# Gate columns moved behind the first two chunk batches, chunk preparation opened on other memory, in a hybrid GDN/retention block on one core

## The chip, the cores and the metric

One core of one Trainium2 chip. The metric is the time of one execution on the device, in microseconds. The engines are TensorE (PE in the profile; PEld are its weight loads), VectorE (DVE), ScalarE (ACT), GpSimd (POOL) and SyncE (SP, which here only issues transfers). Each engine runs its own instructions in order; a scheduler that works at build time has put them in that order, from a model of the engines.

## The reference

One layer, D_MODEL 1024, 1024 latent tokens behind 256 context tokens, all in float32. The modulated, normalized tokens h go through one input projection, whose columns are split; the first half of the heads is a bidirectional gated delta rule (GDN), the second half retention with rotary embedding:

```python
p = (h @ w_in).astype(f32)
qkv_a, z, ab, rq, rk, rv, rg = jnp.split(p, splits, axis=-1)
qkv_a = short_conv(qkv_a, cw)                  # 5 taps, then silu
q = l2_normalize(q) * (HEAD_DIM ** -0.5);  k = l2_normalize(k)
g_f = -A[0] * jax.nn.softplus(a_f + dtb[0])    # and g_b, backward
o_f = gated_delta_rule(q, k, v, g_f, jax.nn.sigmoid(b_f))
...
G = jnp.cumsum(gc, axis=-1)                    # in each chunk
A = jnp.where(strict, jnp.einsum('nbhid,nbhjd->nbhij', kb, kc) * decay, 0.0)
sol = lax.linalg.triangular_solve(A + I, rhs, lower=True, unit_diagonal=True)
...
o_gdn = rms_norm(o_f + o_b) * jax.nn.silu(z)
o_ret = head_group_norm(r_f + r_b) * jax.nn.silu(rg)
x = x + g1 * (y @ w_out);  x = x + g2 * swiglu(modulate(rms_norm(x), sh2, sc2))
```

The gates g1, g2 and the shifts and scales come from adaLN: silu(c) times a 1024 x 6144 matrix. After it a final RMSNorm.

## The kernel before, in words

**Tiles.** The 1280 tokens are ten tiles of 128, two of context and eight latent (LT = 8, TT = 10). h lies in SBUF transposed, as hhi and hlo, its fp32r parts; each product of the projection is three matmuls (hhi·whi, hhi·wlo, hlo·whi). *Token-major* columns (`token_major`, L371 to L373) come in ten groups of 256 columns, 24 matmuls per token tile; the result is emptied into a buffer res by `finish` and stored (L387). Groups 0, 1 are the retention values rv, 2 to 5 rk and rq (rope), 6, 7 the gate columns rg (emptied with a Silu, `fin_gate`, L532), 8, 9 the columns z. *Channel-major* columns (`conv_block`, L611 to L613) are twelve heads of 128 for GDN: 4 to 7 k, 0 to 3 q, 8 to 11 v. One head has chunks of 256, 512 and 512 tokens, each 24 matmuls into a bank of PSUM of the two that are called b (b2 in the program); ScalarE empties each twice, into u and, times the middle tap, into y (L614, L615); VectorE adds the other taps (L621); a Silu ends it (L624).

**The order of the program** around the change: rv; `ada_rest(2, half)` for both halves; the gates chain; four k heads, each with an `ada_rest` and `kstat`; four q heads, the first two with an `ada_rest`; gate columns; chunk batches 0 and 1 (`solve`); four v heads; batch 2; the merges; z. `ada_rest` makes 512 columns of adaLN: four loads of 512 KB (adaw2, two buffers, SP's queue, L495), eight products on VectorE into acc (L497, L499), then a matmul gr (L504 or L509). The gates chain is: av from xa (the 16 gate columns of rv's group 0), softplus, g, the prefix sums G by a matmul with the triangle tri (L582, L583), its transpose GT (L595), neG, gl and kds by three exponentials (L589 to L593), and the store of G to memory as grow_d.

`solve(b)` runs `pre(t)` for the tiles of a batch and then `invert(b)`. `pre` loads the head's keys kc and queries qc from memory (SP), makes kk (L705), the transposed query qt (L710) and kq (L715) on PE, loads G's rows (gw), masks them on GpSimd, puts them through Exp, multiplies (ut, sp on VectorE) and stores both. `invert` inverts the 32 x 32 triangular blocks of a batch row by row on VectorE (X, tmp; L765, L767) and stores the blocks (xd, L771). `merge` (L807, L814 and others; tile m) loads them into U and t (L787, L788) and puts the blocks together with small matmuls. The v heads are turned by PE (vT, L856), scaled on ScalarE into vt (L859, two buffers) and stored.

**Memory.** Pools are opened and closed on two stacks, so what opens later lies on what was closed. Pool W (two buffers) holds the weights of the convolutions and of groups 0, 8 and 9; pool W2 the weights of groups 1, 6 and 7, xa, and the four result buffers of rv; R2 holds the buffers of `ada_rest` and `kstat`; GU, GI and GP those of the chunk preparation and the inverses. Before, W2 and R2 both live from the value columns until the gate columns are done, and GU, GI and GP open behind them (L685 to L693).

Of the kernel before, what the change touches and what calls it, by code (L numbers as in the profile page):

```python
# [17 lines left out]
P = 128  # L18
# [5 lines left out]
TT = NTOK // P  # L24
# [14 lines left out]
def build(nc, tc, ap, dbg=None, stop=None, marks=None):  # L39
    root = ExitStack()  # L40
    V, S, G, T, SY = nc.vector, nc.scalar, nc.gpsimd, nc.tensor, nc.sync

    def pool(name, bufs=1, side=None, space=None):
        kw = {}
        if side is not None:
            kw["side"] = side
        if space is not None:
            kw["space"] = space
        if space is not DRAM:
            kw["reuse_waits"] = "tile"  # L50
# [8 lines left out]
    def close(p):  # L59
        p_close.pop(id(p)).close()  # L60
# [29 lines left out]
    def bank_a(name):  # L90
        return bank("pa", name)

    def bank_b(name):
        return bank("pb", name)
# [96 lines left out]
    try:  # L191
# [20 lines left out]
        W = pool("w", bufs=2)  # L212
# [14 lines left out]
        xts, raws, small = {}, {}, {}  # L227
# [4 lines left out]
        W2 = None  # L232
# [127 lines left out]
        def tm_weights(g, kh, pl, q=S):  # L360
            return weights(ap["wt"][g, :, 4 * kh:4 * kh + 4, :], [4, 256], V, pl, q, raws.get((g, kh)), g == 0)

        def tm_bank(g):
            return bank_a("tm")[:, 0:WIDE if g == 0 else 256]

        def tm_half(o, w, kh, t):

            tsl = slice(t * P, (t + 1) * P)
            whi, wlo = w
            for k in range(4 * kh, 4 * kh + 4):  # L370
                T.matmul(o, hhi[:, k, tsl], whi[:, k % 4, :], start=(k == 0), stop=False)  # L371
                T.matmul(o, hhi[:, k, tsl], wlo[:, k % 4, :], start=False, stop=False)  # L372
                T.matmul(o, hlo[:, k, tsl], whi[:, k % 4, :], start=False, stop=(k == KT - 1))  # L373
# [5 lines left out]
        def tm_store(g, t, o, finish, store, pl):  # L379
            early = g < 2  # L380
            res = (W2 if early else R1).tile([P, 256], F32, tag="res", name="res", bufs=4 if early else 2)
            finish(t, o[:, 0:256], res)
            if g == 0:
                S.activation(xa[:, t, :], o[:, 256:WIDE], AF.Copy)
            nm, c0 = GROUPS[g // 2], (g % 2) * 256
            dst = zd[t - 2, :, c0:c0 + 256] if nm == "z" else rd[t, :, RD[nm], c0:c0 + 256]
            store.dma_start(dst, res)  # L387

        def token_major(g, tiles, finish, store, pl, q=S):

            w = [tm_weights(g, kh, pl, q) for kh in range(2)]

            for p in range(0, len(tiles), 2):
                pair = [(t, tm_bank(g)) for t in tiles[p:p + 2]]
                for kh in range(2):
                    for t, o in pair:
                        tm_half(o, w[kh], kh, t)
                for t, o in pair:
                    tm_store(g, t, o, finish, store, pl)
# [48 lines left out]
        W2 = pool("w2", bufs=2)  # L448
        xa = W2.tile([P, TT, 16], F32, tag="xa", name="xa", bufs=1)
# [31 lines left out]
        checkpoint("h")  # L481


        R2 = pool("r2", bufs=2)
        ada2 = C.tile([P, 2, KT], F32, tag="ada2", name="ada2")
        grow = [dr.tile([1, D], F32, tag="grow%d" % i, name="grow%d" % i) for i in range(2)]

        def ada_rest(c, half):

            c0 = c * D + half * 512  # L490
            acc = R2.tile([P, 512], F32, tag="acc", name="acc", bufs=1)
            for k in range(KT):
                if k % 2 == 0:
                    w = R2.tile([P, 2, 512], F32, tag="adaw2", name="adaw2", bufs=2)
                    SY.dma_start(w, ap["ada_w"][k * P:(k + 2) * P, c0:c0 + 512].rearrange("(a p) n -> p a n", p=P))  # L495
# [5 lines left out]
            if c in (2, 5):  # L501
                row = R2.tile([1, 512], F32, tag="row", name="row", bufs=1)
                SY.dma_start(row, ap["adarow"][c0:c0 + 512].unsqueeze(0))
# [12 lines left out]

        nA = R2.tile([P, 8], F32, tag="nA", name="nA", bufs=1)

# [15 lines left out]
        LAT, ALL = list(range(2, TT)), list(range(2, TT)) + [0, 1]  # L534
        for g in range(2):
# [1 line left out]
        checkpoint("rv")  # L537


        GS = pool("gs", side="right")  # L540
        sm = {n: GS.tile([P, TT * 8], F32, tag=n, name=n)
              for n in ("g", "G", "nG", "Gt", "neG", "gl", "beta", "ab", "kds")}
        nk = GS.tile([P, TT, H], F32, tag="nk", name="nk")
        nq = GS.tile([P, LT, H], F32, tag="nq", name="nq")
        cw = GS.tile([P, 12, 5], F32, tag="cw", name="cw")
        SY.dma_start(cw, ap["cw"])
# [8 lines left out]
        def c8(t, d):  # L555
            return slice(t * 8 + d * 4, t * 8 + d * 4 + 4)

        AB = pool("ab", side="right")
        tri = AB.tile([P, 2, P], F32, tag="tri", name="tri")
        SY.dma_start(tri, ap["tri"])  # L560
        CHUNKS = [(0, 256), (256, 512), (768, 512)]
        av = AB.tile([P, 2, TT * 8], F32, tag="av", name="av")
        av3 = av.rearrange("p a (t c) -> p a t c", c=8)
        V.tensor_tensor(av3[:, 0], xa[:, :, 0:8], bc(small["dtb"], [P, TT, 8], 1), ALU.add)
        V.tensor_scalar(av3[:, 1], xa[:, :, 8:16], -1.0, None, ALU.mult)
        S.activation(nA, small["alog"], AF.Exp)
        V.tensor_scalar(nA, nA, -1.0, None, ALU.mult)
        sp = softplus(AB, av.rearrange("p a n -> p (a n)"), 2 * TT * 8, "sp")

        lnb = GS.tile([P, TT, 2, H], F32, tag="lnb", name="lnb")  # L570
        V.tensor_scalar(lnb.rearrange("p t d h -> p (t d h)"), sp[:, TT * 8:], -1.0, None, ALU.mult)
# [1 line left out]
        V.tensor_tensor(sm["g"].rearrange("p (t c) -> p t c", c=8), sp.rearrange("p (t c) -> p t c", c=8),  # L573
                        bc(nA, [P, TT, 8], 1), ALU.mult)
        be = sm["beta"].rearrange("p (t c) -> p t c", c=8)
        S.activation(be, xa[:, :, 8:16], AF.Exp, scale=-1.0)
        V.tensor_scalar(sm["beta"], sm["beta"], 1.0, None, ALU.add)
        V.reciprocal(sm["beta"], sm["beta"])
        ps = bank_b("G")
# [15 lines left out]
        T.transpose(ps[:80, :P], sm["G"], ident)  # L595
        gT = AB.tile([80, P], F32, tag="gT", name="gT")
        V.tensor_copy(gT, ps[:80, :P])
        SY.dma_start(grow_d, gT)
        close(AB)
        CV = pool("cv", side="right")  # L600
# [25 lines left out]
        def newy():  # L626
            return CV.tile([P, NTOK], F32, tag="y", name="y", bufs=3)
# [3 lines left out]
        def kstat(h, y):  # L631

            cut = ((0, 4), (4, 4), (8, 2))
            ps = [bank_b("kt") for _ in cut]
            kts = [R2.tile([P, 2, 4, P], F32, tag="kt", name="kt", bufs=3) for _ in cut]
            for (t0, n), pt, kt in zip(cut, ps, kts):
# [4 lines left out]
            V.tensor_scalar(nk[:, :, h], nk[:, :, h], EPS, None, ALU.add)  # L641
            rk2 = R2.tile([P, TT], F32, tag="rk2", name="rk2", bufs=2)
            V.reciprocal(rk2, nk[:, :, h])
# [25 lines left out]

        lnk = log(GS, nkf, TT * H, "ln").rearrange("p (t h) -> p t h", h=H)  # L670
        nG4 = sm["nG"].rearrange("p (t d h) -> p t d h", d=2, h=H)
# [11 lines left out]
                        y[:, NCTX:].rearrange("p (t j) -> p t j", j=P))  # L683

        checkpoint("q")  # L685
        for g in (6, 7):
            token_major(g, LAT, fin_gate, S, W2, SY)
        checkpoint("rg")
        close(R2)
        close(W2)  # L690
        GU = pool("gu")
        GI = pool("gi")
        GP = pool("gp")  # L693
# [147 lines left out]
        def solve(b):  # L841
            for t in BATCH[b]:
                pre(t)
            checkpoint("pre%d" % b)
            invert(b)
            checkpoint("inv%d" % b)

        solve(0)
        solve(1)
        for h in range(H):  # L850
            y = newy()
            conv_block(8 + h, y, False)
            for t0, n in ((0, 2), (2, 4), (6, 4)):
                ps = bank_a("vT")
                for t in range(t0, t0 + n):
                    T.transpose(ps[:, (t - t0) * P:(t - t0 + 1) * P], y[:, t * P:(t + 1) * P], ident)  # L856
                vt = CV.tile([P, 4, P], F32, tag="vt", name="vt", bufs=2)
                for t in range(n):
                    S.activation(vt[:, t], ps[:, t * P:(t + 1) * P], AF.Copy, scale=sv3[:, t0 + t, h:h + 1])  # L859
                S.dma_start(vd[t0:t0 + n, :, h, :].rearrange("t p j -> p t j"), vt[:, :n])  # L860
# [687 lines left out]
        for m in (1, 6, 2, 7, 5, 4, 3):  # L1548
            gs = [list(range(j, min(j + 2, FH))) for j in range(4 if m == 1 else 0, FH, 2)]
# [103 lines left out]
```

## Time and profile before

| | us |
|---|---|
| three timed runs, median (range) | 1481.48 (1479.01 to 1484.4) |
| profiled execution, span | 1479.4 |
| PE busy in the span | 1400.0 (95%) |
| VectorE busy | 969.2 (66%) |
| ScalarE busy | 613.4 (41%) |
| GpSimd busy | 590.5 (40%) |

The times are those of three runs; of the profiled execution itself the profile gives the span, from the first to the last instruction. In a timeline a row is start, duration, engine, line of the kernel, operation, result <- operands, shapes, count, and in brackets the idle time ahead of it with what ended it. In the view of waits a row is the engine and its instruction, what it waited for, and the total, the number and the longest of those waits. "issue" stands where the profile shows nothing that was waited for.

### The profile page before, as it was taken

To read this page: it belongs to the slowest core of one execution; us is meant where nothing else is said; L and a number is where in the kernel's file an instruction comes from. 1 tells how busy PE (TensorE), PEld (TensorE's weight loads), DVE (VectorE), ACT (ScalarE), POOL (GpSimd) and SP (SyncE) were. 2 spreads that over 40 slices of the span, in tenths; PEclk is the share of its full clock that TensorE was granted. 3 is DMA by queue.
4 is the path that set the end of the run, shared out by engine and by line. 5 is a ranking of instruction groups with operands and counts; after the bars stand their busy time and mean duration, and the time that the engine had idled before them with its cause. 6 is when DMAs were issued, how large, how long until landed. Compare 5 with 4: busy or idle time off the path is not lost.

```text
span 1479.4 us, 24109 instructions
## 1 busy us (share of the span) xinstructions
PE 1400.0 (95%) x8919; PEld 1203.0 (81%) x8919; DVE 969.2 (66%) x1856; ACT 613.4 (41%) x1326; POOL 590.5 (40%) x501
## 2 busy tenths in 40 slices
PE   7999999987789999899699899999999999999997
PEld 2898888976789999799588688877888888788886
DVE  6566789289782535579777877646555564657577
ACT  5643564687333111245534533223333332444444
POOL 0120010243201354244144688899555553325321
PEclk9999999999899999999899999999999999999999
DMA  8536686688878723996633265765222242785863
GB/s 323 210 106 203 189 250 199 223 263 279 269 196 271 272 72 118 416 372 204 215 114 115 86 226 208 260 238 178 107 108 107 107 150 76 234 280 193 305 206 114
DMA packets 176565, 298.14 MB, mean 202 GB/s; under 512 B 43496, under 2 KB 93880, under 8 KB 172096
## 3 DMA queue, kind: packets, MB, share of 16 engines
q1 hardware_dynamic: 124896, 253.17, 49.7%
q10 hardware_dynamic: 49072, 35.83, 7.8%
q0 software_dynamic: 2480, 7.60, 1.4%
q8 instruction: 70, 1.15, 0.3%
q14 instruction: 47, 0.39, 0.1%
HBM read 206.60 MB, written 89.96 MB: 200 GB/s over the span
## 4 chain that ended last, share of the span: by engine, by line
PE 55%; POOL 6%; DMA 6%; issue 3%; DVE 2%; ACT 2%; SPq 0%; ACTq 0%; POOLq 0%; DVEq 0%
PE ffn L1344 7%; PE ffn L1342 6%; PE ffn L1343 6%; PE fo L1470 5%; PE fo L1468 5%; PE fo L1469 5%; PE tm L371 3%; PE tm L372 3%; PE tm L373 3%; PE op L1201 2%; PE op L1203 2%; PE op L1202 2%; DMA wd<-tw 1%; POOL ws L1315 1%; PE up L929 1%
## 5 line engine op out<-in xcount | busy, mean ns | idle before, releaser
L371 PE MATMUL tm<-whi,hhi 128*128 128x256 f32 (+1 forms) x704 | 201.5, 290 | 6.1 <-ACT vt L859 2.9
L372 PE MATMUL tm<-wlo,hhi 128*128 128x256 f32 (+1 forms) x704 | 200.8, 287 | 0.3 <-DVE wlo L345 0.3
L373 PE MATMUL tm<-whi,hlo 128*128 128x256 f32 (+1 forms) x704 | 198.6, 286 | 0.0
L371 PEld LDWEIGHTS tm<-whi,hhi 128*128 128x128 f32 x704 | 134.2, 192 | 10.3 <-ACT vt L859 3.1
L344 ACT ACTIVATE whi<-wraw 128x512 fp32r<-128x512 f32 (+2 forms) x98 | 75.2, 771 | 159.7 <-PE ffn L1343 81.9
L1344 PE MATMUL ffn<-t,wlo 128*128 128x512 f32 x352 | 137.1, 390 | 1.4 <-DVE wlo L345 1.4
L1342 PE MATMUL ffn<-t,whi 128*128 128x512 f32 x352 | 137.0, 390 | 1.3 <-ACT whi L344 1.3
L1343 PE MATMUL ffn<-t,whi 128*128 128x512 f32 x352 | 137.0, 389 | 0.0
L372 PEld LDWEIGHTS tm<-wlo,hhi 128*128 128x128 f32 x704 | 135.2, 192 | 2.2 <-issue 0.9
L373 PEld LDWEIGHTS tm<-whi,hlo 128*128 128x128 f32 x704 | 134.3, 192 | 0.7 <-DVE hlo L314 0.2
L344 ACT ACTIVATE whi<-ws 128x512 fp32r<-128x512 f32 x88 | 55.6, 632 | 173.0 <-PE ffn L1343 123.7
L345 DVE TENSOR_TENSOR wlo<-ws,whi 128x512 fp32r<-128x512 f32 x88 | 95.1, 1081 | 45.7 <-ACT whi L344 45.3
L1468 PE MATMUL fo<-whi,ahi 128*128 128x512 f32 x308 | 119.3, 389 | 0.7 <-ACT ahi L344 0.7
L1469 PE MATMUL fo<-wlo,ahi 128*128 128x512 f32 x308 | 119.9, 389 | 0.0
L1470 PE MATMUL fo<-whi,alo 128*128 128x512 f32 x308 | 119.0, 390 | 0.0
L345 DVE TENSOR_TENSOR wlo<-wraw,whi 128x512 fp32r<-128x512 f32 (+2 forms) x92 | 103.4, 1125 | 23.4 <-ACT whi L344 23.2
L1342 PE MATMUL ffn<-b,whi 128*128 128x512 f32 x264 | 103.9, 394 | 4.3 <-ACT whi L344 4.3
L1344 PE MATMUL ffn<-b,wlo 128*128 128x512 f32 x264 | 103.7, 393 | 0.7 <-DVE wlo L345 0.7
L1343 PE MATMUL ffn<-b,whi 128*128 128x512 f32 x264 | 103.7, 393 | 0.0
L612 PE MATMUL b<-hlo,whi 128*128 128x512 f32 (+1 forms) x256 | 94.7, 370 | 0.0
L613 PE MATMUL b<-hhi,wlo 128*128 128x512 f32 (+1 forms) x256 | 94.5, 369 | 0.0
L611 PE MATMUL b<-hhi,whi 128*128 128x512 f32 (+1 forms) x256 | 94.2, 368 | 0.0
(446 smaller groups left out, 3443.7 us busy)
## 6 DMA issues: line engine op xcount, KB each, us to landing
adaw<-ada_w SPq DMA_DIRECT2D x48, 512.0 KB, 4.8
pk<-sd SPq DMA_DIRECT2D x16, 1536.0 KB, 11.6
wraw<-wfi SPq DMA_DIRECT2D x44, 512.0 KB, 3.9
ar<-ad SPq DMA_DIRECT2D x33, 512.0 KB, 4.8
w<-wfo SPq DMA_DIRECT2D x22, 512.0 KB, 5.7
wd<-tw SPq DMA_DIRECT2D x11, 1024.0 KB, 4.8
ad<-act SPq DMA_DIRECT2D x20, 512.0 KB, 3.1
raw<-wd SPq DMA_DIRECT2D x20, 512.0 KB, 4.9
```

What stands on the lines that cost most here:

```text
L344: S.activation(hi, raw, AF.Copy)
L345: e.tensor_tensor(lo, raw, hi.bitcast(F32), ALU.subtract)
L371: T.matmul(o, hhi[:, k, tsl], whi[:, k % 4, :], start=(k == 0), stop=False)
L372: T.matmul(o, hhi[:, k, tsl], wlo[:, k % 4, :], start=False, stop=False)
L373: T.matmul(o, hlo[:, k, tsl], whi[:, k % 4, :], start=False, stop=(k == KT - 1))
L612: T.matmul(o, whi[:, k, :], hl, start=False, stop=False)
L1342: T.matmul(o, whi[:, k, :], xhi(xn, slice(0, 4), k), start=(first and k == 0), stop=False, **kw)
L1343: T.matmul(o, whi[:, k, :], xlo(xn, slice(0, 4), k), start=False, stop=False, **kw)
L1344: T.matmul(o, wlo[:, k, :], xhi(xn, slice(0, 4), k), start=False, stop=(k == 3), **kw)
L1468: T.matmul(po[g][i], ahi[:, ts], whi, start=(j == 0 and not kw), stop=False, **kw)
L1469: T.matmul(po[g][i], ahi[:, ts], wlo, start=False, stop=False, **kw)
L1470: T.matmul(po[g][i], alo[:, ts], whi, start=False, stop=(j == FH - 1), **kw)
```

## The change

Three edits. First, the pools GS and AB open, and tri, av and its two operations stand, ahead of `ada_rest(2, ·)`; then W2 is closed, and R2 is opened behind that, so R2 lies where W2 was. The exponential for beta now reads av instead of xa, which is closed by then. Second, the two groups of gate columns go behind `solve(0)` and behind `solve(1)`, and take their weights from pool W instead of W2, still on SP's queue. Third, W2 is therefore not open when GU, GI and GP are opened; what these lie on has been free since the value columns, apart from what R2 covers.

```diff
+        GS = pool("gs", side="right")
+        AB = pool("ab", side="right")
+        tri = AB.tile([P, 2, P], F32, tag="tri", name="tri")
+        SY.dma_start(tri, ap["tri"])
+        av = AB.tile([P, 2, TT * 8], F32, tag="av", name="av")
...
+        V.tensor_tensor(av3[:, 0], xa[:, :, 0:8], bc(small["dtb"], [P, TT, 8], 1), ALU.add)
+        V.tensor_scalar(av3[:, 1], xa[:, :, 8:16], -1.0, None, ALU.mult)
+        close(W2)
         R2 = pool("r2", bufs=2)
...
-        S.activation(be, xa[:, :, 8:16], AF.Exp, scale=-1.0)
+        S.activation(be, av3[:, 1], AF.Exp)
...
         checkpoint("q")
-        for g in (6, 7):
-            token_major(g, LAT, fin_gate, S, W2, SY)
-        checkpoint("rg")
         close(R2)
-        close(W2)
         GU = pool("gu")
...
         solve(0)
+        token_major(6, LAT, fin_gate, S, W, SY)
         solve(1)
+        token_major(7, LAT, fin_gate, S, W, SY)
+        checkpoint("rg")
```

The scheduler orders all engines anew. Line numbers differ by a few: L611 to L613 of before are L612 to L614 after, L504 is L513, L582 is L583, L705 is L702, and so on.

The first place is PE in the first k head, behind its second chunk. The names are tm, a tile of gate columns; gr, the matmul that ends a half of `ada_rest(2, ·)`; G, the prefix sums; GT, G transposed; b2, a chunk of a convolution. Before, around the second gr:

```order
L371 MATMUL tm_2477<-whi_2409,hhi_86 128x256
L504 MATMUL gr_1273<-acc_1256,ones_81 1x512
L372 MATMUL tm_2477<-wlo_2410,hhi_86 128x256
L373 MATMUL tm_2477<-whi_2409,hlo_87 128x256
L371 MATMUL tm_2477<-whi_2409,hhi_86 128x256
L372 MATMUL tm_2477<-wlo_2410,hhi_86 128x256
L582 MATMUL G_1335<-g_1282,tri_1301 128x40 x2
L583 MATMUL G_1335<-g_1282,ones_81 128x80
```

After, from the end of the second chunk to the start of the third:

```order
L614 MATMUL b2_1393<-hhi_86,wlo_1360 128x512
L513 MATMUL gr_1262<-acc_1245,ones_81 1x512
L513 MATMUL gr_1285<-acc_1268,ones_81 1x512
L583 MATMUL G_1336<-g_1291,tri_1232 128x40 x2
L584 MATMUL G_1336<-g_1291,ones_81 128x80
L596 MATMUL GT_1349<-ident_65,G_1292 80x128
L612 MATMUL b2_1420<-hhi_86,whi_1359 128x512
```

Six tiles' worth of gate columns, 135 matmuls, stood between the second chunk and the third, and gr, G and GT were strewn among them; now both gr, G and GT follow one another, and no gate column is near.

The second place is SP's queue at the loads of adaLN columns for these two halves. adaw2 are the loads, row the adaLN bias and grow0 the finished half row. Before:

```order
L495 DMA adaw2_1234<-ada_w 128x2x512
L495 DMA adaw2_1238<-ada_w 128x2x512
L503 DMA row_1251<-adarow 1x512
L546 DMA cw_1293<-cw 128x60
L560 DMA tri_1301<-tri 128x256
L495 DMA adaw2_1242<-ada_w 128x2x512
L495 DMA adaw2_1246<-ada_w 128x2x512
L495 DMA adaw2_1257<-ada_w 128x2x512
L495 DMA adaw2_1261<-ada_w 128x2x512
L354 DMA wraw_2647<-wt 128x1024
```

After:

```order
L487 DMA tri_1232<-tri 128x256
L554 DMA cw_1302<-cw 128x60
L504 DMA adaw2_1246<-ada_w 128x2x512
L504 DMA adaw2_1250<-ada_w 128x2x512
L512 DMA row_1263<-adarow 1x512
L504 DMA adaw2_1254<-ada_w 128x2x512
L504 DMA adaw2_1258<-ada_w 128x2x512
L504 DMA adaw2_1269<-ada_w 128x2x512
L504 DMA adaw2_1273<-ada_w 128x2x512
```

The order of the loads is the same, and the loads of gate-column weights (wraw from wt) among them are gone; but the two buffers of adaw2 now lie where W2's weights and results were.

The third place is PE behind the last v head, where kk, qt and kq belong to the last two tiles of the third batch, vT to the last two v heads, and tm_4968 is the first tile of z. Before, from the last convolution matmul:

```order
L613 MATMUL b2_3980<-hhi_86,wlo_3920 128x512
L705 MATMUL kk_4055<-kc_4053 128x128 x3
L856 MATMUL vT_3889<-ident_65,y_3791 128x128 x2
L856 MATMUL vT_3896<-ident_65,y_3791 128x128 x4
L856 MATMUL vT_3907<-ident_65,y_3791 128x128 x4
L705 MATMUL kk_4055<-kc_4053 128x128
L710 MATMUL qt_4062<-ident_65,qc_4060 128x128 x4
L715 MATMUL kq_4071<-qc_4060,kc_4053 128x128 x4
L705 MATMUL kk_4114<-kc_4112 128x128 x4
L710 MATMUL qt_4121<-ident_65,qc_4119 128x128 x4
L715 MATMUL kq_4130<-qc_4119,kc_4112 128x128 x4
L856 MATMUL vT_4016<-ident_65,y_3918 128x128 x2
```

After:

```order
L614 MATMUL b2_3980<-hhi_86,wlo_3920 128x512
L707 MATMUL qt_4121<-ident_65,qc_4119 128x128 x4
L712 MATMUL kq_4130<-qc_4119,kc_4112 128x128
L856 MATMUL vT_3889<-ident_65,y_3791 128x128 x2
L856 MATMUL vT_3896<-ident_65,y_3791 128x128 x4
L856 MATMUL vT_3907<-ident_65,y_3791 128x128 x4
L712 MATMUL kq_4130<-qc_4119,kc_4112 128x128 x3
L856 MATMUL vT_4016<-ident_65,y_3918 128x128 x2
L856 MATMUL vT_4023<-ident_65,y_3918 128x128 x4
L856 MATMUL vT_4034<-ident_65,y_3918 128x128 x4
L371 MATMUL tm_4968<-whi_4956,hhi_86 128x256
```

Both kk, the first qt and the first kq have moved ahead into the convolutions; one qt, one kq and the vT of two heads are left behind the last convolution.

More of the change, by code (lines that the diff above doesn't have):

```diff
@@ L481, in build @@
         checkpoint("h")
+        GS = pool("gs", side="right")
[3 more added lines that the diff above has]
+        av = AB.tile([P, 2, TT * 8], F32, tag="av", name="av")
+        av3 = av.rearrange("p a (t c) -> p a t c", c=8)
+        V.tensor_tensor(av3[:, 0], xa[:, :, 0:8], bc(small["dtb"], [P, TT, 8], 1), ALU.add)
+        V.tensor_scalar(av3[:, 1], xa[:, :, 8:16], -1.0, None, ALU.mult)
+        close(W2)
         R2 = pool("r2", bufs=2)
@@ L537, in build @@
         checkpoint("rv")
-        GS = pool("gs", side="right")
         sm = {n: GS.tile([P, TT * 8], F32, tag=n, name=n)
@@ L556, in c8 @@
             return slice(t * 8 + d * 4, t * 8 + d * 4 + 4)
-        AB = pool("ab", side="right")
-        tri = AB.tile([P, 2, P], F32, tag="tri", name="tri")
-        SY.dma_start(tri, ap["tri"])
         CHUNKS = [(0, 256), (256, 512), (768, 512)]
[L562 to L565, printed above, removed]
         S.activation(nA, small["alog"], AF.Exp)
```

## Prediction

> **What bounds the kernel now.** I read the page first, then busy time by stage, then the waits of TensorE (PE), then the timelines at the two places that the change touches. The page gives the span of the one profiled execution, on which the whole sum is made:
>
> ```profile
> span 1479.4 us, 24109 instructions
> ```
>
> The three timed runs have a median of 1481.5, 2.1 above this span, and I carry that distance over unchanged. Busy time by stage has the columns stretch, length, PE, PE weight loads, VectorE (DVE), ScalarE (ACT), GpSimd (POOL), granted PE clock, DMA share and GB/s:
>
> ```profile
> 120.00:140.00 20.00, 20.00 (x154) 18.61 (x153) 12.94 (x32) 7.01 (x14) 0.00 (x0) 1.00 0.66 211
> 320.00:340.00 20.00, 17.13 (x100) 14.96 (x99) 18.49 (x35) 16.05 (x43) 7.49 (x7) 0.91 0.74 242
> 360.00:380.00 20.00, 8.92 (x40) 8.45 (x41) 17.27 (x31) 12.56 (x43) 4.93 (x5) 0.59 0.81 268
> 380.00:400.00 20.00, 17.15 (x130) 16.95 (x130) 14.24 (x37) 3.51 (x9) 4.29 (x4) 0.89 0.95 305
> 400.00:420.00 20.00, 15.78 (x410) 14.61 (x409) 18.41 (x48) 5.51 (x9) 0.00 (x0) 0.96 0.91 208
> 440.00:460.00 20.00, 17.10 (x373) 16.20 (x372) 9.43 (x22) 7.87 (x14) 0.00 (x0) 0.91 0.82 222
> ```
>
> PE has no gap at all where the gates and the first convolution run (120 to 140). It has gaps in the chunk preparation and the inverses (320 to 460), worst in 360 to 380, where its clock also falls to 0.59. So PE sets the time, and the change can only win what PE waits there. Those waits, 280 to 480, with total, times and longest:
>
> ```profile
> PE vT L856 <- ACT y L624: 9.1, 3, 8.5
> PE kk L705 <- issue: 7.5, 2, 6.8
> PE m L814 <- issue: 6.1, 2, 3.2
> PE tm L371 <- ACT vt L859: 2.9, 1, 2.9
> PE qt L710 <- issue: 2.5, 1, 2.5
> ```
>
> That is 28.1 us, the most that an earlier chunk preparation can give back, apart from clock.
>
> **The change, part by part.** *The first k head.* These are PE's rows around the gates, before:
>
> ```profile
> 111.05 0.28 PE L611 MATMUL b<-hhi,whi 128*128 128x256 f32 x1
> 115.04 0.40 PE L611 MATMUL b<-hhi,whi 128*128 128x512 f32 x1
> 120.61 0.28 PE L371 MATMUL tm<-whi,hhi 128*128 128x256 f32 x1
> 126.94 1.02 PE L504 MATMUL gr<-acc,ones 128*1 128x512 f32 x2
> 128.46 0.54 PE L582 MATMUL G<-g,tri 128*128 128x40 f32 x4
> 131.86 0.27 PE L595 MATMUL GT<-ident,G 128*80 128x128 f32 x1
> 138.62 0.40 PE L611 MATMUL b<-hhi,whi 128*128 128x512 f32 x1
> ```
>
> The head's first chunk starts at 111.05, its second at 115.04, and at 120.61 PE goes over to gate columns (tm), because the third chunk has no PSUM bank until ScalarE has emptied the first. It starts at 138.62. The 18.0 us between are filled by 135 gate-column matmuls; less about 2.2 for the gr, G and GT matmuls among them, these are 15.8 us of work. The change takes them away from here. By the new order, PE meets both gr matmuls, G and GT in a row behind the second chunk, then the third chunk, and nothing else. One gr of 1.02 that lay inside the first chunk now lies behind the second, so PE arrives at 120.6 − 1.0 = 119.6 and stands still until the chain of the second gr is done. What is in that chain, on SP's queue, then by landing, on VectorE and on ScalarE:
>
> ```profile
> 117.65 2.23 SPq L495 DMA_DIRECT2D adaw<-ada_w  x2
> 124.08 2.08 SPq L495 DMA_DIRECT2D adaw<-ada_w  x2
> 131.23 1.68 SPq L495 DMA_DIRECT2D adaw<-ada_w  x2
> ```
>
> Landing times of the same stretch (100 to 150; KB each, median us to landing):
>
> ```profile
> adaw<-ada_w SPq DMA_DIRECT2D x13, 512.0 KB, 4.4
> rd<-res ACTq DMA_DIRECT2D x10, 128.0 KB, 4.1
> ```
>
> ```profile
> 107.14 2.41 DVE L564 TENSOR_TENSOR av<-xa,dtb 128x80 f32<-128x80 f32 x1
> 123.31 0.74 DVE L499 SCALAR_TENSOR_TENSOR acc<-adaw,csl,acc 128x512 f32<-128x512 f32 x1
> 129.29 0.30 DVE L585 COPY G<-G 128x40 f32<-128x40 f32 x2 [0.23 <-PE G L583]
> ```
>
> ```profile
> 112.75 0.33 ACTq L387 DMA_DIRECT2D rd<-res  x1
> 130.70 0.27 ACT L593 ACTIVATE kds<-kds 128x80 f32<-128x80 f32 x1 [0.64 <-DVE kds L592]
> 134.98 0.39 ACT L614 ACTIVATE u<-b 128x256 f32<-128x256 f32 x1 [0.40 <-ACT res L532]
> 136.09 0.70 ACT L615 ACTIVATE y<-b,cw 128x512 f32<-128x512 f32 x1
> ```
>
> The two column halves of the adaLN gate row need eight loads of 512 KB through two buffers, and sixteen VectorE products. Before, most of these loads ran under the value columns. Now the pool of their buffers opens on the memory that the value columns' weights and result buffers held, and the second buffer lies over the last results, so its first load waits for the last value store: issued at 112.75 plus 0.33, landed 4.1 later (the median of those rows), 117.2. The first load of that buffer has landed 4.4 later, 121.6. VectorE does the whole gates chain first (av starts at 107.14, and its operations add up to about 10 us, so 117); that is hidden. Then there are three more steps of two loads each. Before, such steps were 6.4 and 7.2 apart (117.65, 124.08, 131.23); a buffer that is emptied at once needs 4.4 + 2 × 0.74 = 5.9. I take 6.1: 121.6 + 18.3 = 139.9, plus two products, 141.4, less some 1.5 because the first buffer runs ahead of the second: 140. From the second gr on, before, kds ended 4.0 later (126.94 to 130.97), u of the first chunk takes 0.39, and y of it 0.47 as its row would be between u's 0.39 and the 512-wide 0.70: third chunk at 140 + 0.2 + 4.0 + 0.9 + 0.5 for the next adaLN products ahead of G's copies on VectorE, about **146**. The store order on ScalarE adds nothing: behind the last value store only these activations stand. Its bounds: at VectorE's own pace, sixteen products from 117 on, at most 0.74 each, end at 128.8, so 134.5; at 7.2 a step, 150. Of 119.6 to 146, 26.4 us, gr, G and GT fill 3.3: PE stands still for **23 us** where it had no gap.
>
> *What restarts cold.* After the 2.9 wait in 380 to 400 the clock row reads 0.89, which over 20 us is 2.2 lost. I take 2.0 for the restart at 146, between 1 and 4.
>
> *The gate columns* themselves cost the same 15.8 us later; all 384 of their matmuls now stand among the first chunk preparations. Moving them costs nothing by itself, and is paid as the hole above.
>
> *Up to the z columns.* These rows, before, are the end of the last v head:
>
> ```profile
> 351.67 0.39 PE L613 MATMUL b<-hhi,wlo 128*128 128x512 f32 x1
> ...
> 354.75 1.06 PE L715 MATMUL kq<-qc,kc 128*128 128x128 f32 x8
> 362.56 2.04 PE L705 MATMUL kk<-kc 128*128 128x128 f32 x8 [6.76 <-issue]
> 375.86 2.40 PE L856 MATMUL vT<-ident,y 128*128 128x128 f32 x10 [8.52 <-ACT y L624]
> 377.91 0.56 PE L371 MATMUL tm<-whi,hhi 128*128 128x256 f32 x1
> ```
>
> ```profile
> 371.15 1.27 DVE L621 SCALAR_TENSOR_TENSOR y<-u,cw,y 128x1022 f32<-128x1022 f32 x1
> ```
>
> ```profile
> 373.25 1.28 ACT L624 ACT_TABLE_LOAD   x1
> 374.54 1.27 ACT L624 ACTIVATE y<-y 128x1280 f32<-128x1280 f32 x1
> 376.59 0.62 ACT L859 ACTIVATE vt<-vT,svy 128x128 f32<-128x128 f32 x2 [0.78 <-PE vT L856]
> ```
>
> From the third chunk (138.6) to the first z column (377.9) are 239.3 us. In them PE waits 6.8 (kk) and 8.5 (vT) here and 4.9 in small pieces before (the rest of the rows of waits: vT 0.6, kk 0.7, qt 2.5, and 1.1 in others). Low clock costs 1.8 in 320 to 340 (20 × 0.09), 2.4 in the last kk, qt and kq (eight kk take 2.04, eight kq at full clock 1.06), 0.8 in vT. Work at full clock: 239.3 − 20.2 − 5.0 = 214.1. Afterwards it is 214.1 + 15.8 = 229.9, of which 4.3 (one qt, one kq, two vT) stand behind the last convolution matmul. The small waits and the kk wait I take as gone: kk, qt and kq have their loads long before. The vT wait stays, as PE has nothing else ahead of z. From the last convolution matmul to z: u and y of a 512-wide chunk (0.6 + 0.7), four taps of 1.27, some 2.9 of preparation and inverse operations that the order leaves between the taps, the silu (1.27), first vT (0.3) and its vt (0.62): 11.5. The table load of 1.28 runs under the taps.
>
> New waits, 6.0 in all by estimate: 1.5 at the gr matmul two places into the second k head, whose four loads come two steps of 6.1 behind 140, against 146 + 5.6; and 4.5 in the mixed stretch, where ScalarE now alternates Silu for gate columns with Exp for the preparation (three to four table loads of 1.28). Bounds 0 and 12. A rule speaks for the upper end: the Trainium skill, "ScalarE: Activation LUTs", section "What ACT_TABLE_LOAD costs", gives 1.28 for the load and 1.38 more for a drain, 2.66 a switch. By it, as an estimate, this term would be 5 us more and the time 1499 (rival 4). The trace speaks against it: the load at 373.25 ends at 374.53, and the silu starts at 374.54.
>
> So z starts at 146 + 2.0 + (229.9 − 4.3) + 6.0 + 11.5 = 391.1 instead of 377.9: **+13**.
>
> *Behind z.* The waits of m and tm, 9.0, and clocks of 0.89, 0.96 and 0.91 remain roughly: the second inverse now ends sooner behind z, but the loads of the first inverse's diagonal blocks (U) come behind the stores of the second one on SP's queue, some 4 us that merge(0) waits. I take −1, between −8 and +8. The first part of the change (tri and av earlier, the exponential from av) moves a dozen small operations under the value columns; it costs nothing while PE is full, and under 3 us if not. **Sum: +12.5**, a span of 1491.9, and **1494** for the median. Its own range, from 142 to 150 for the third chunk and 3 to 10 for the new waits: 1487 to 1502.
>
> **Rivals.**
> 1. *Faster: the hole closes.* If the eight loads keep pace with VectorE (store landed by 115, loads in 3 us), the third chunk starts at 134.5, ahead of 138.6. With no new waits, z starts at 134.5 + 2.0 + 225.6 + 11.5 = 373.6, −4.3, and with the m waits (6.1) gone through earlier inverses −10: 1471. For it: nothing else holds the loads. Against: 4.4 for landing, and the steps of 6.4 and more. It decides at the third chunk: below about 139 without new waits the kernel is faster. 0.18.
> 2. *A wash.* The hole closes to 134.5, but the 6.0 and the waits behind z come: 373.6 + 6.0 − 377.9 − 1 = +1, 1482. 0.10.
> 3. *Slower still: the merges wait.* U of the first inverse stands on SP behind the second inverse's stores. If VectorE needs for the rest of that inverse, mixed with the third batch's preparation, ten us more than the merge is from z, PE stands in front of m L814 for them: +12.5 + 10, 1504. For it: SP is in order. Against: DVE has less left to do then. 0.14.
> 4. *Every switch on ScalarE costs double.* A drain as long as the load behind each new table would make the 4.5 above 9.5, as the page named there has it: 1499. Against it stand the rows named there. 0.02.
> 5. *The preparation doesn't open earlier.* If kc and qc wait for stores of the last q head anyway, the kk and small waits (11.7) and their clock (4.2) stay: +12.5 + 14, 1508. 0.06.
>
> **How the numbers follow.** The forecast has 0.50, the rivals 0.18, 0.10, 0.14, 0.02, 0.06. A measurement here can tell 0.3%, 4.4 us. Faster is rival 1, 0.18; within it is rival 2, 0.10; the rest is slower, 0.72. The range must leave out no more than 0.2: from 1475 (a part of rival 1 lies below) to 1507 (most of rival 3 inside).
>
> **What would show it.** Right: in the new profile PE has a wait of 20 us or more ahead of gr or of the third chunk between 119 and 146, released through acc by adaw loads; the kk wait of 6.8 is gone; z starts near 391; the vT wait stays at 6 to 9. Wrong: PE full from 110 to 140, or the third chunk before 139; or z within 3 us of 377.9; or waits of m above 12.

## The result, and the profile after

The changed kernel takes 1500.3 us (median of 4 runs, 1497.6 to 1500.9) against 1481.8; the ratio is 1.0113, 95% interval 1.0095 to 1.0131, so 1.1% slower. The forecast was 1494 with a range of 1475 to 1507. Among the experiments, one execution of the changed kernel with fewer taps took 2331 us at a granted clock of 0.555, beside three of 1504 to 1510, and is left out of its ratio.

```profile
span 1498.8 us, 24114 instructions
```

PE around the gates, after the change (line 513 is gr, 612 the first matmul of a convolution chunk):

```profile
126.08 1.87 PE L513 MATMUL gr<-acc,ones 128*1 128x512 f32 x2 [6.18 <-DVE acc L508]
138.09 1.86 PE L513 MATMUL gr<-acc,ones 128*1 128x512 f32 x2 [10.14 <-DVE acc L508]
144.13 0.79 PE L612 MATMUL b<-hhi,whi 128*128 128x512 f32 x1 [1.57 <-ACT y L616]
```

PE arrives at 126.08 − 6.18 = 119.9, waits for the two sums of adaLN products, and goes on with the third chunk at 144.13; each gr takes 1.87 where it took 1.02 before. VectorE in turn waits for the loads:

```profile
119.03 1.54 DVE L508 SCALAR_TENSOR_TENSOR acc<-adaw,csl,acc 128x512 f32<-128x512 f32 x2 [1.30 <-DMA adaw<-ada_w]
124.48 1.54 DVE L508 SCALAR_TENSOR_TENSOR acc<-adaw,csl,acc 128x512 f32<-128x512 f32 x2 [1.29 <-DMA adaw<-ada_w]
133.85 1.54 DVE L508 SCALAR_TENSOR_TENSOR acc<-adaw,csl,acc 128x512 f32<-128x512 f32 x2 [2.43 <-DMA adaw<-ada_w]
136.49 1.54 DVE L508 SCALAR_TENSOR_TENSOR acc<-adaw,csl,acc 128x512 f32<-128x512 f32 x2 [1.11 <-DMA adaw<-ada_w]
```

The division that explains most is into three stages, each between the same two places of the program in both kernels: from 119.9 to the third chunk of the first k head, from there to the first z column, and from there to the end. Busy time of the engines in these, first before, then after (length; PE, weight loads, VectorE, ScalarE, GpSimd; clock, DMA share, GB/s):

```profile
119.90:138.62 18.72, 18.72 (x149) 17.57 (x147) 11.69 (x30) 6.79 (x14) 0.00 (x0) 1.00 0.64 201
138.62:377.91 239.29, 219.11 (x1263) 189.37 (x1262) 181.59 (x289) 148.75 (x422) 52.49 (x45) 0.96 0.73 229
377.91:1479.40 1101.49, 1055.08 (x6822) 914.88 (x6820) 700.09 (x1392) 393.26 (x772) 519.11 (x435) 0.98 0.56 194
```

```profile
119.90:144.13 24.23, 5.67 (x12) 1.67 (x12) 14.10 (x26) 1.39 (x6) 0.00 (x0) 0.57 0.58 176
144.13:403.36 259.23, 235.85 (x1397) 205.34 (x1397) 200.17 (x341) 167.00 (x439) 55.86 (x49) 0.96 0.77 236
403.36:1498.80 1095.44, 1055.00 (x6822) 913.85 (x6820) 682.25 (x1345) 392.63 (x771) 516.00 (x432) 0.98 0.56 192
```

PE's idle time is length less busy time. It is 0, 20.2 and 46.4 before, and 18.6, 23.4 and 40.4 after. The first stage is 5.5 longer although the gate columns that filled it have left it; the second is 19.9 longer, of which 16.7 is busy time, nearly all that moved work, and 3.2 is idle time; the third is 6.0 shorter. Together 19.4, the difference of the spans. VectorE's work has moved ahead of z as well: it is busy for 18.6 more in the second stage and for 17.8 less in the third.

So the earlier preparation took nothing from the second stage. What PE waits for there, after the change (144 to 403):

```profile
PE vT L856 <- ACT y L625: 15.4, 3, 10.3
PE b L612 <- ACT y L616: 4.1, 2, 2.5
PE kk L702 <- ACT qt L709: 1.9, 2, 1.1
PE tm L371 <- ACT res L541: 1.7, 2, 0.9
PE qt L707 <- issue: 1.4, 1, 1.4
```

The waits of kk and qt, 10.0 before and all called "issue", are 3.3. In their place the waits for y, a v head's convolution on its way through VectorE and ScalarE, rose from 9.1 to 17.9 (15.4 for vT and 2.5 for b; the other 1.6 of b's 4.1 stands ahead of the third chunk itself). The waits called "issue" were not for transfers. Before the change, VectorE's product ut, which reads the previous kk out of its PSUM bank, ended at 362.46, and the kk that had waited 6.8 started at 362.56:

```profile
361.18 1.28 DVE L730 TENSOR_TENSOR ut<-kk,e 128x512 f32<-128x512 f32 x2
```

Each wait of kk or qt over 0.4 us that is called "issue" between 119 and 405 us, 28 in the fourteen traces, ends 0.10 behind such a product (27 times ut, once sp). So these were waits for VectorE, before the change already.

Of the waits for y, the three earlier ones, 7.6 together, go by ScalarE: it stands idle for 4.6 and 1.6 ahead of an Exp of the preparation that needs GpSimd's mask, which waits for a load of G's rows (gw), and the convolution's operations stand behind that Exp. The last and longest goes by VectorE; on PE and VectorE:

```profile
388.17 0.39 PE L614 MATMUL b<-hhi,wlo 128*128 128x512 f32 x1
389.06 1.25 PE L856 MATMUL vT<-ident,y 128*128 128x128 f32 x10
401.31 2.39 PE L856 MATMUL vT<-ident,y 128*128 128x128 f32 x10 [10.33 <-ACT y L625]
403.36 0.56 PE L371 MATMUL tm<-whi,hhi 128*128 128x256 f32 x1
```

```profile
391.49 1.22 DVE L345 TENSOR_TENSOR wlo<-wraw,whi 128x1024 fp32r<-128x1024 f32 x1
392.63 0.39 DVE L764 TENSOR_TENSOR X<-X,tmp 128x231 f32<-128x231 f32 x1
392.94 1.28 DVE L622 SCALAR_TENSOR_TENSOR y<-u,cw,y 128x1022 f32<-128x1022 f32 x1
394.13 1.28 DVE L729 TENSOR_TENSOR sp<-kq,e 128x512 f32<-128x512 f32 x2
395.33 0.40 DVE L762 TENSOR_TENSOR tmp<-L,X 128x240 f32<-128x240 f32 x1
395.64 1.28 DVE L622 SCALAR_TENSOR_TENSOR y<-u,cw,y 128x1023 f32<-128x1023 f32 x1
...
398.68 1.28 DVE L622 SCALAR_TENSOR_TENSOR y<-u,cw,y 128x1022 f32<-128x1022 f32 x1
```

VectorE has no gap here: a split of weights for z (wlo), the score products (sp) and the second inverse (tmp, X) stand among the four taps, so the last tap ends at 399.96, and z starts 14.8 after the last convolution matmul has ended (403.36 less 388.56). The ten turns vT take 2.39 behind the wait and 1.25 at 389.06 without one.

### The profile page after: what moved, and what is told of

Same layout as the page of the kernel before. It is cut to its first block, busy times and chain, and to the rows that moved or that the text cites. A ratio compares the mean times of both kernels' runs of the same rounds, so it can differ in the third digit from the quotient of the medians.

```text
span 1498.8 us, 24114 instructions
## 1 busy us (share of the span) xinstructions
PE 1405.7 (94%) x8919; PEld 1202.6 (80%) x8919; DVE 965.3 (64%) x1856; ACT 622.3 (42%) x1332; POOL 590.5 (39%) x501
## 5 line engine op out<-in xcount | busy, mean ns | idle before, releaser
L1469 PE MATMUL fo<-wlo,ahi 128*128 128x512 f32 x308 | 119.9, 389 | 0.0
L612 PE MATMUL b<-hhi,whi 128*128 128x512 f32 (+1 forms) x256 | 95.8, 374 | 4.1 <-ACT y L616 4.1
L614 PE MATMUL b<-hhi,wlo 128*128 128x512 f32 (+1 forms) x256 | 95.5, 374 | 0.4 <-DVE wlo L345 0.4
L613 PE MATMUL b<-hlo,whi 128*128 128x512 f32 (+1 forms) x256 | 95.2, 372 | 0.0
```

Source lines behind the costliest of these rows:

```text
L612: T.matmul(o, whi[:, k, :], hh, start=(k == 0), stop=False)
L1469: T.matmul(po[g][i], ahi[:, ts], wlo, start=False, stop=False, **kw)
```

## The experiments

Four theories. **A**: the loss is the hole in the first k head, and it reaches the end in full. **B**: it is VectorE in the v heads, where inverses and taps meet. **C**: the stretch from the preparation to the merges has a pace of its own and swallows what PE wins or loses ahead of it. **D**: ScalarE, alternating between Silu and Exp, holds up the early preparation. Ratios are to the kernel before, run on the same chip.

### The length of the hole: half and one and a half times the loads

```diff
-            for k in range(KT):
+            for k in range(KT if c != 2 else 4):
```

> As after the change, but each half of adaLN's first gate row takes only four of its eight row blocks (so the residual gate is a partial sum): two loads a half instead of four, all else in its order. The third chunk comes at about 132 instead of 144. Theory A (the hole is on the path): nearly all of the 12 us reach the end, 1489 (1486 to 1492). Theory C (the stretch from the chunk preparation to the merges is paced by its own chains, transfers and stores among them, and takes up what PE wins ahead of it): 4 us or less reach the end, 1496 or more.

```diff
-            for k in range(KT):
+            for kk in range(KT if c != 2 else 12):
+                k = kk % KT
```

> The reverse: each half takes twelve row blocks (the first four twice, so the gate is a wrong sum): six loads a half instead of four, the third chunk at about 156. Theory A: 12 us more, 1512 (1509 to 1516). Theory C: 6 us or less, 1506 or below.

With half the loads the ratio is 1.0043 (1.0023 to 1.0062), with one and a half times 1.0185 (1.0154 to 1.0215). The third chunk, first with half, then with more:

```profile
131.16 0.80 PE L612 MATMUL b<-hhi,whi 128*128 128x512 f32 x1 [1.57 <-ACT y L616]
```

```profile
153.63 0.80 PE L613 MATMUL b<-hhi,whi 128*128 128x512 f32 x1 [1.57 <-ACT y L617]
```

and what the two gr wait for there, with more (total, times, longest):

```profile
PE gr L514 <- DVE acc L509: 26.2, 2, 15.3
```

Up to z these keep PE's order matmul for matmul, and move only the hole: it ends at 131.2, 144.1 and 153.6, and the ratios times 1482 give 1488, 1499 and 1509. So −13.0 at the hole is −10 at the end, +9.5 is +11, each give or take some 4 to 5 by the intervals. A holds, about one for one; C does not. From the third chunk to z the three take 259.7, 259.2 and 261.1. Behind z the traces differ more (1102.9, 1095.4 and 1091.7): the traced execution with half the loads was the longest of eight, the one with more the shortest of four, and some of the order there differs. So the slope is read from the ratios, and a few microseconds behind z in a single trace mean little.

### The hole taken away

```diff
-        for g in range(2):
-            ada_rest(2, g)
...
-            if h < 2:
-                ada_rest(5, h)
+            ada_rest(5 if h < 2 else 2, h % 2)
```

> Both halves of adaLN's first gate row are made with the last two q heads instead of ahead of the gates chain. Theory A (the loss is the hole in the first k head, where TensorE waits for gr behind eight loads): G comes at about 120, the third chunk near 125 instead of 144, the hole is 6 us or less, and the time falls by 19, to 1481 (1477 to 1486). Theory B (the loss is VectorE in the v heads, where inverses and taps now meet): the hole closes too, but TensorE then waits as much more for the silu of the v heads; the time stays above 1494.

The ratio is 1.0051 (1.0035 to 1.0067), median 1489.5: 11 us below the changed kernel, and still 7 above the one before. PE has hardly a wait at the first head, and the old one at the last:

```profile
122.97 0.50 PE L610 MATMUL b<-hhi,whi 128*128 128x512 f32 x1 [2.30 <-ACT y L614]
388.09 2.40 PE L853 MATMUL vT<-ident,y 128*128 128x128 f32 x10 [11.20 <-ACT y L623]
```

The hole ends 21.2 earlier, but only about half of that shows in the medians, less than the slope above. The sixteen adaLN products now lie with the last q heads, PE waits 3.3 there for a split of weights, and the first kk comes at 273.8, where the changed kernel has it at 264.1; which of these costs how much isn't separated. The median lies between the two expectations: A is right on the hole, and wrong that nothing else is lost. The traced execution was the shortest of the ten (1483.7).

### The memory under the buffers

```diff
-        close(W2)
         R2 = pool("r2", bufs=2)
...
         close(R2)
+        close(W2)
```

> The gate columns stay behind the first two batches with weights from the convolutions' pool, but the old weight pool is closed only where it was, so the adaLN buffers don't lie on its memory. Theory A: the loads run under the value columns again, the second gr is ready at about 127 as before the change, the third chunk starts at 132, and the hole is 12 instead of 24: 1488 (1484 to 1493). If the memory under the buffers doesn't matter, only the missing gate columns do: 1500. Theory B: 1498 or more, since VectorE's work in the v heads is unchanged.

The third chunk comes at 131.3, as expected (132):

```profile
131.34 0.80 PE L611 MATMUL b<-hhi,whi 128*128 128x512 f32 x1 [1.57 <-ACT y L615]
```

But the ratio is 1.0109 (1.0077 to 1.0140), no better than the changed kernel. The profiled execution was the shortest of four, 1491.5; the others took 1499 to 1501, so its trace can't show where the 12.8 us went. That stays open.

### The gate columns back ahead of the preparation

```diff
+        for g in (6, 7):
+            token_major(g, LAT, fin_gate, S, W, SY)
         close(R2)
...
-        token_major(6, LAT, fin_gate, S, W, SY)
...
-        token_major(7, LAT, fin_gate, S, W, SY)
```

> The gate columns go back ahead of the chunk preparation, with weights from the convolutions' pool; the memory edits stay. Theory A: the hole is the same 24, and the preparation opens late again: 1502 (1497 to 1509). Theory B: the inverses move away from the v heads' taps again, the waits for the silu fall back to those of before, and the time falls to 1490.

The ratio is 1.0174 (1.0152 to 1.0196). The hole is as long as before (third chunk at 142.9) and the wait of kk is back:

```profile
349.86 2.05 PE L705 MATMUL kk<-kc 128*128 128x128 f32 x8 [6.69 <-issue]
400.06 2.40 PE L856 MATMUL vT<-ident,y 128*128 128x128 f32 x10 [11.77 <-ACT y L625]
```

Against this kernel, with nearly the same hole, putting the gate columns behind the batches gains 0.6% (the two intervals lie apart). In the traces none of that lies between the third chunk and z (259.3 here, 259.2 in the changed kernel); behind z it is 1099.3 against 1095.4. A was right to 5 us; B, which expected a gain, was wrong, for the wait for y is 11.8 with the gate columns ahead too.

### Four buffers

```diff
-                    w = R2.tile([P, 2, 512], F32, tag="adaw2", name="adaw2", bufs=2)
+                    w = R2.tile([P, 2, 512], F32, tag="adaw2", name="adaw2", bufs=4)
```

> Four buffers instead of two for the adaLN loads, all else as after the change. Theory A with the buffers as the cause of the pace: the sixteen products run at VectorE's pace from 117 on, the third chunk starts at 135 to 137, and the time falls by 8, to 1492 (1488 to 1496). If landing itself sets the pace (queue or memory), the steps stay and the time is 1499 to 1502. Theory B: no more than 3 us gained in the end.

The third chunk comes at 138.3, 5.9 earlier, so the pace was set by the buffers only in part, and the ratio is 1.0167 (1.0141 to 1.0193), worse than every expectation. Two waits behind z are longer than any of their kind in the changed kernel:

```profile
418.97 0.58 PE L371 MATMUL tm<-whi,hhi 128*128 128x256 f32 x1 [6.34 <-ACT vt L859]
448.48 0.26 PE L814 MATMUL m<-xt,U 32*32 32x32 f32 x1 [5.27 <-issue]
```

More buffers take 8 KB a partition more and give the scheduler another order further on, so this run tells of the loads' pace, and not cleanly of what that is worth.

### Fewer taps, after and before

```diff
-            for i, e in ((0, V), (1, V), (3, V), (4, V)):
+            for i, e in (((1, V), (3, V)) if b >= 8 else ((0, V), (1, V), (3, V), (4, V))):
```

> As after the change, but the v heads' convolution leaves out its two outer taps (half of the tap work of four heads, some 14 us of VectorE; the v part of the output is that of three taps). Theory B (after the change VectorE bounds the v heads, since the inverses stand among the taps): the waits of vT and of the next chunk for the silu fall from 18 us to under 9 and the time falls by 8 to 12, to 1490. If VectorE isn't what the v heads wait for: 3 us at most, 1498.

> The same two taps left out of the kernel before the change, as a control. Theory B: there only the last v head waits for its silu (8.5 us), so 3 to 5 us come off: 1478. If as much comes off as from the changed kernel (8 or more), VectorE bounded the v heads already, and the change made nothing worse there.

In the changed kernel the ratio is 1.0152 (1.0117 to 1.0187), slower, not faster; in the kernel before it is 0.9942 (0.9924 to 0.9960), 8.6 us faster, more than the 3 to 5 expected. The last wait for y, and the largest wait behind z, with fewer taps after the change:

```profile
399.44 2.40 PE L856 MATMUL vT<-ident,y 128*128 128x128 f32 x10 [9.27 <-ACT y L625]
432.51 0.58 PE L371 MATMUL tm<-whi,hhi 128*128 128x256 f32 x1 [6.13 <-ACT res L541]
```

and with fewer taps before it:

```profile
370.06 2.40 PE L856 MATMUL vT<-ident,y 128*128 128x128 f32 x10 [3.04 <-ACT y L624]
```

B as stated has fallen. By the control, VectorE bounded the v heads already before the change: the last wait for y falls from 8.5 to 3.0. After the change, the scheduler moves operations of the second inverse up into the place of the missing taps: the last chunk is emptied at 392.1, and its first tap starts at 395.3, with five operations of the inverse and a split of weights in between. The last tap starts 252.1 behind the third chunk instead of 254.6, and z comes at 401.5 − 144.6 = 256.9 instead of 259.2. What little that is goes again behind z (1103.4 to the end instead of 1095.4). So it is the order of VectorE's work in the changed kernel, with other operations ahead of the last taps, and not the sum of the taps, that keeps the wait; why the stage behind z got longer I can't show.

### Batch 1 and gate group 7 behind the v heads

Both start from the kernel without the hole; the first moves `solve(1)` and group 7, the second group 7 alone.

```diff
-        solve(1)
-        token_major(7, LAT, fin_gate, S, W, SY)
...
+        solve(1)
+        token_major(7, LAT, fin_gate, S, W, SY)
         close(CV)
```

> The adaLN row with the last q heads (as in the first experiment), and batch 1 with gate group 7 behind the v heads instead of ahead of them. Theory B: the second inverse leaves the taps alone, PE has 192 gate-column matmuls (23 us) behind the last vT, and the time falls below both kernels: 1476 (1470 to 1483). Rival: the inverse of batch 1 comes later than its merge is due, PE waits at m for it, and the time is 1490 or more.

> The adaLN row with the last q heads, and only gate group 7 behind the v heads; batch 1 stays ahead of them. Theory B: VectorE has the same work among the taps and the v heads lose their filler, so PE waits for the silu in each of them, 25 us in all instead of 13; what the gate columns fill later doesn't give that back: 1489 to 1497. Rival (PE only lacked work in the right place): 1482 or less.

The ratios are 1.0139 (1.0109 to 1.0169) and 1.0090 (1.0060 to 1.0119). In the first, gate and z columns meet on PE, and it waits for their results to be emptied and at the merges; in the second, the v heads lack filler, and kk waits instead:

```profile
380.81 0.58 PE L371 MATMUL tm<-whi,hhi 128*128 128x256 f32 x1 [5.11 <-ACT res L541]
436.47 0.25 PE L811 MATMUL m<-xt,U 32*32 32x32 f32 x1 [4.21 <-issue]
```

```profile
342.67 2.05 PE L699 MATMUL kk<-kc 128*128 128x128 f32 x8 [5.03 <-issue]
```

The rival was right on the first, though its waits at m are only part of it. On the second, the time lies at the upper end of B's range, but not for B's reason: PE waits for y there once, 2.1 us, and not 25. Both also wait 4.8 near 255 for a split of weights, which the changed kernel doesn't.

### Early preparation without a hole

```diff
-        for g in (6, 7):
-            token_major(g, LAT, fin_gate, S, W2, SY)
+        token_major(6, LAT, fin_gate, S, W2, SY)
         close(R2)
         close(W2)
...
         solve(0)
+        token_major(7, LAT, fin_gate, S, W, SY)
         solve(1)
```

> The kernel before, with gate group 6 left in its place (weights from the old pool, so TensorE has it as work in the first k head), the old pool closed behind it, and only group 7 put behind batch 0 with weights from the convolutions' pool. Theory A: no hole, third chunk at 138.6 as before, and the preparation opens 23 us of gate columns earlier: 1475 (1470 to 1480). Theory C: the gain is taken up behind it: 1480 to 1486. If it loses more than 4 us, early preparation itself costs.

The ratio is 1.0021 (0.9999 to 1.0042): no gain, and perhaps a small loss. There is no wait at the third chunk; what PE waits for up to z:

```profile
139.78 0.40 PE L611 MATMUL b<-hhi,whi 128*128 128x512 f32 x1
```

```profile
PE vT L856 <- ACT y L624: 16.4, 4, 13.1
PE b L611 <- ACT y L615: 5.8, 2, 3.3
PE kk L703 <- issue: 2.8, 1, 2.8
PE qt L708 <- issue: 2.0, 1, 2.0
```

This separates the two halves of the change, and C's expectation is the one that was met. Gate group 6 fills the first head as it did, and group 7 alone opens the preparation earlier. The waits of kk and qt fall from 10.0 to 4.8, and those for y rise from 9.1 to 22.2. From the third chunk to z it takes 246.4 instead of 239.3, and behind z 1096.9 instead of 1101.5: the same exchange as in the changed kernel, with more lost ahead of z. So the time that the hole loses reaches the end, and the time that early preparation was to win does not. No version beat the kernel before with all of its work done.

### ScalarE's switches

```diff
-            S.activation(res, o, AF.Silu)
+            S.activation(res, o, AF.Copy)
```

> As after the change, but ScalarE empties the gate columns and the z columns with a plain copy instead of a Silu (the output lacks that Silu), so that 15 table loads of 1.28 fall away between 259 and 314, where Silu and Exp alternate; TensorE's order is the same. Theory D (the switching on ScalarE holds up the early chunk preparation, and so the first inverse): the first inverse starts at 297 to 300 instead of 309, the waits of TensorE between 280 and 400 shrink, and the time falls by 6 to 12, to 1491. Rival (VectorE's work in the v heads takes up whatever comes earlier, or the loads run in idle time): the inverse starts sooner, but the time moves by 3 us or less, 1498. If each switch cost a drain as long as its load besides, the inverse would start some 20 us sooner, limited by its loads.

The ratio is 1.0086 (1.0070 to 1.0101), some 4 us below the changed kernel, between the two expectations; the intervals just overlap, so this size is less sure than the others. The third chunk comes at 142.7, 1.4 earlier, and VectorE starts the first inverse at 305.2 instead of 309.3. A switch and a switch back, in the changed kernel:

```profile
282.18 1.28 ACT L541 ACT_TABLE_LOAD   x1
283.48 0.38 ACT L541 ACTIVATE res<-tm 128x256 f32<-128x256 f32 x1
283.88 1.28 ACT L723 ACT_TABLE_LOAD   x1
285.17 0.40 ACT L723 ACTIVATE e<-e,nG 128x128 f32<-128x128 f32 x1
```

The loads between the third chunk and z, by the line that causes them (723 is the preparation's Exp, 541 the gate columns' Silu; busy time, mean ns, idle time ahead), in the changed kernel:

```profile
L723 ACT ACT_TABLE_LOAD x9 | 11.5, 1283 | 1.7 <-ACT res L541 1.2 <-ACT y L625 0.4
L541 ACT ACT_TABLE_LOAD x7 | 9.0, 1283 | 0.1
```

and without the Silu, where line 541 has none:

```profile
L723 ACT ACT_TABLE_LOAD x2 | 2.6, 1283 | 0.5 <-ACT y L625 0.4
```

The convolutions' Silu has three more in both. So 14 loads fewer, 18 us of ScalarE, are worth about 4 in the end, of which 1.4 lies ahead of the third chunk, where no load was taken away; from there to z it is 256.3 instead of 259.2. The change itself adds fewer than fourteen: there are ten loads in this stretch before it and nineteen after. D is true in kind and a fifth of the loss at most.

## Why the prediction was right, and where it was not

**The hole** was right: the loads of adaLN's gate row set it, with no gate column to fill it. The third chunk came at 144.1, forecast 146. VectorE's pairs of products, one pair a load, start 2.6 to 2.8 apart, 5.5 for the two buffers (119.03 to 124.48), where 6.1 was taken; a load landed in a median of 3.7, where 4.4 was taken. PE stood still for 18.6, less than the 23 forecast: the chain was 2 us shorter, and gr, G and GT took 5.7 and not 3.3. That the hole is paid at the end is shown by half and one and a half times the loads.

**Moving the gate columns costs nothing by itself**: 16.7 of busy time more up to z, 15.8 forecast. Some 1.5 of it is the restart behind the hole: the third chunk's first eight matmuls take 3.4 instead of 1.9.

**Up to the z columns** the working failed at "The small waits and the kk wait I take as gone" and at the term for new waits, 6.0. The kk and qt waits did fall, 10.0 to 3.3. But the reason given, that their loads are there long before, missed what they waited for: VectorE's ut, in the kernel before already. The forecast counted VectorE only behind the last convolution, and the change put 18.6 us more of VectorE's work into this stretch. Nor did it count the v heads' emptying and silu, which stand behind the preparation's Exp on ScalarE. PE waits 23.4 where the forecast left 13 (6.0, and about 7 of the 11.5 to z). From the last convolution to z it took 14.8 instead of 11.5: 1.5 more of VectorE's other work (4.4 for 2.9), 1.2 more for the last turns and their scaling, 0.6 more for ScalarE, which splits a weight ahead of u. From the third chunk to z 259.2, forecast 245.1, so 14 short: 10 of that is idle time, and 4 is busy time, as the 5.0 that low clock cost here before was taken off and didn't go (granted clock 0.96 before and after). ScalarE's switches, 4.5 forecast, were at most 4, and for fourteen loads and not four.

**Behind z** the forecast took −1, and it was −6.0, all of it idle time of PE (46.4 to 40.4), with the same 6822 matmuls. The waits of m fell from 6.1 to 4.3, that of tm for vt from 2.9 to 0.6; the store order on SP that rival 3 feared didn't show. VectorE has 17.8 us less to do there. But this is one execution of each kernel, and the traces with half and more loads differ by 11 in the same stage.

In sum −1.9, +14.1 and −5.0 against the terms (13.2 to z and −1 behind it, 12.2, which the forecast gives as 12.5): +19.4 in the span. The sign and the hole were right; what early preparation does up to z was not, and two errors of opposite sign partly cancelled, so that the time is only 6 us from the forecast is in part luck. Of the signs that it named, the kk wait did go and the hole was there, with 18.6 for the 20 asked; z came at 403.4 and not near 391, and the last wait for y was 10.3 and not 6 to 9.

Of **the rivals**, the first two needed a third chunk before 139; it came at 144. With half the loads it came at 131, and the kernel was still slower than before (1.0043), so that even then the first would not have come true. The third needed longer waits of m, and they fell. The fourth, a drain behind each table load, has no room in the rows of the last experiment: each activation starts 0.01 to 0.02 behind the end of its load. The 1.28 of the Trainium skill, "ScalarE: Activation LUTs", section "What ACT_TABLE_LOAD costs", is what the trace has; its 1.38 for a drain isn't there. The fifth needed a preparation that opens no earlier; the first kk came at 264.1, and at 276.1 before. (Its terms, 11.7 and 4.2, add up to 15.9 and not to 14.)

## What to carry to other kernels

Before moving filler work away from a place, read what it covers: here 16 us of gate columns hid a chain of eight loads, and the chain was paid in full. Before counting a wait as won, find what ends it: here the waits called "issue" ended with VectorE's reading of a PSUM bank, and earlier preparation put others in their place, no shorter, behind VectorE's taps and behind ScalarE's Exp. To learn whether a stall is on the path, change its length and nothing else, in both directions; pools and program order move too much with them.

## What the runs showed of the hardware that I had not expected

After waits of 6 to 10 us both gr took 1.87 instead of 1.02, and over the hole the granted clock reads 0.57. In the run with half the loads a gr behind a wait of 0.4 took 1.02 and one behind a wait of 4.4 took 1.86. The restart behind the hole cost some 1.5 on the third chunk (granted clock 0.53 from 144.13 to 147.54), since it fell on few matmuls. Fourteen table loads, 18 us of ScalarE's time in a stretch where it alternates, moved the end by only about 4.
